# The opening of a two-layer diffusion backbone step: order of the first loads, and three table operations put behind the last modulated x

## Chip, cores and metric

The kernel runs on one core of one Trainium2 chip. The metric is device time in microseconds (us) of one execution; lower is better. A run's time is the span of the profiled work plus what lies around it.

## The reference, cut to what matters

Each layer first makes a modulation out of a condition vector, six vectors of 1024 (shift, scale, gate, twice), and applies shift and scale to its input:

```python
def modulation(cond, w, b):
    return jnp.split((jax.nn.silu(cond) @ w + b)[:, None, :], 6, axis=-1)

mp = modulation(c_ctx[None, :], w_ada[l], b_ada[l])   # 128 prompt tokens
ms = modulation(c, w_ada[l], b_ada[l])                # 256 latent tokens
hp = xp * (1 + mp[1]) + mp[0]
hs = xs * (1 + ms[1]) + ms[0]
# layer 0: windowed attention and a bidirectional recurrence behind one projection of h
... = jnp.split(h @ w_in, EVEN_SPLIT, axis=-1)
```

In layer 0 queries and keys of the latent tokens are rotated with a table of cosines and sines (`rope`); in layer 1 the same rotation follows an RMS norm with the gains `d_q_norm` and `d_k_norm`. Everything is float32; d_model is 1024, there are 384 tokens, and `w_ada` is 1024 x 6144 a layer.

## The kernel before, in words

h is kept with the features on the partitions, in eight blocks of 128 features, each as a high part `hH` and a low part `hL` (float32r), and each weight tile is split in the same way (`wload`, lines 113 to 124: ACT writes `wh` on line 122, DVE writes `wl` on line 123). A product is then three matmuls.

**The opening (function `mixer_ab`, lines 979 to 1070).** Before anything can be projected, shift and scale of layer 0 must exist. That is done in four steps u = 0..3, each for 256 of the 1024 features:

- `ada_first(u)` (lines 293 to 317) is a generator. Up to its first `yield` it issues eight loads of 256 KB of `w_ada` (line 299), into four tiles of a ring of five (`raws`). Then TensorE makes 64 small products with the transposed condition `cT` (line 307), in portions of 32, 16 and 16; DVE adds the bias (`ada_row`, line 311); TensorE transposes the row (`ada_t`, line 314); DVE writes shift and scale into `modT` (lines 316, 317).
- `x_load(hf)` (line 990) loads a half of x (512 features of 3 x 128 tokens) in three transfers; `x_turn(k0, k1)` (line 996) transposes a block of 128 features with three transposes on TensorE (line 1000) and copies the result out, even blocks on ACT (line 1004), odd ones on DVE (line 1002).
- `h_part(u)` (line 1009) writes `hH` (ACT, line 1015), the unrounded h (DVE, line 1016) and `hL` (DVE, line 1018) of two blocks.
- `proj_load(u)` and `proj_part(u, i, js)` (lines 1022, 1027) load three tiles of `w_in_ab` and add to six accumulators; six matmuls a call (lines 1036 to 1038).

In the loop over u the parts of the projection of step u stand alternately with the portions of `ada_first(u + 1)`: the first part, 32 products, the second, 16, the third, 16 and the row, the fourth, then the transposed row; the last two parts behind it. In the kernel before, the second half of x is loaded and transposed in step u = 0.

**What sets the order.** Inside `tc.manual_schedule(engines={ET.SP, ET.PE})` the instructions of SP's queue and of TensorE stay in the order of the program. ACT, DVE and POOL are ordered by a planner that simulates a timeline when the kernel is built; `ahead(part)` gives it a priority offset (`"rope": 1000`). On the chip each engine works off its queue in order, and an instruction that waits holds up all behind it. Every load is issued by SP.

**The tables.** Behind the loop, `load_consts` (line 138) loads the sink logits, norm gains and the rotation tables, and makes `nsink` (DVE, line 144); `load_masks` (line 149) loads the band mask and rounds it into `bmaskR` (ACT, line 155) and casts `lmask` (POOL). `fold_rope` (line 1209) multiplies the rotation table with a gain for layer 1 (DVE, lines 1214 and 1216: `tb`, with `gdk`); it is called at line 1469 with the priority of `"rope"`, and its first result is read in layer 1.

**The start.** Lines 82 to 95 load the identity and both condition vectors, take the SiLU on ACT (line 87), transpose on TensorE and copy to `cT` on DVE (line 91). ACT loads a function table ahead of the rounding of `ident` (line 151) and another one ahead of the SiLU.

Of the kernel before, what the change touches and what calls it, by code (L numbers as in the profile page):

```python
# [9 lines left out]
F32 = mybir.dt.float32  # L10
F32R = mybir.dt.float32r
U8 = mybir.dt.uint8
AF = mybir.ActivationFunctionType
ALU = mybir.AluOpType
# [6 lines left out]
P = 128  # L21
D = 1024
# [19 lines left out]
def tile_backbone_step(ctx, tc, I, O):  # L42
    nc = tc.nc
# [30 lines left out]
    dma = nc.sync.dma_start  # L74

    @contextmanager
    def ahead(part, more=0):
        with tc.high_priority(offset=AHEAD[part] + more):
            yield


    ident = const.tile([P, P], F32, name="ident")
    dma(out=ident, in_=I["k_ident"])
    cond = adas.tile([P, 256], F32, tag="row", name="cond")[0:16, 0:P]
    dma(out=cond[0:8, :], in_=I["c_ctx"].rearrange("(k p) -> k p", p=P))
    dma(out=cond[8:16, :], in_=I["c"].rearrange("a (k p) -> (a k) p", p=P))
    nc.scalar.activation(cond, cond, AF.Silu)
    p0 = psa.tile([P, 512], F32, tag="psa", name="p_cond")
    nc.tensor.transpose(p0[:, 0:16], cond, ident[0:16, 0:16])
# [2 lines left out]
        out=cT, in_=p0[:, 0:16].rearrange("p (c k) -> p k c", c=2).unsqueeze(2).to_broadcast([P, KD, 16, 2]))  # L92
# [8 lines left out]
    hH = const.tile([P, KD, NTOK], F32R, name="hH")  # L101
    hL = const.tile([P, KD, NTOK], F32R, name="hL")
# [33 lines left out]
    C = {}  # L136

    def load_consts():
        for name, ap, n in (("sink", I["a_sink"], 8), ("gnorm", I["b_gnorm"], P), ("gckv", I["c_kv_norm"], 256),
                            ("gdq", I["d_q_norm"], 64), ("gdk", I["d_k_norm"], 64)):  # L140
            C[name] = const.tile([P, n], F32, name=name)
            dma(out=C[name], in_=ap.to_broadcast([P, n]))
        C["nsink"] = const.tile([P, 8], F32, name="nsink")
        nc.vector.tensor_scalar(out=C["nsink"], in0=C["sink"], scalar1=-1.0, scalar2=None, op0=ALU.mult)
        for name, sh in (("rope", [P, 2, 2, 64]), ("ropec", [P, 2, 2, 32])):
            C[name] = const.tile(sh, F32, name=name)
            dma(out=C[name], in_=I["k_" + name])

    def load_masks(stg, pool):
        C["identR"] = pool.tile([P, P], F32R, name="identR")  # L150
        nc.scalar.activation(C["identR"], ident, AF.Copy)
        C["bmask"] = pool.tile([P, 2, P], F32R, name="bmaskR")
        bmask = stg([P, 2, P], F32, "bmask")
        dma(out=bmask, in_=I["k_band"])
        nc.scalar.activation(C["bmask"], bmask, AF.Copy)
        C["lmask"] = pool.tile([P, 7, P], U8, name="lmask")
        for a, b in ((0, 4), (4, 7)):
            lm32 = stg([P, b - a, P], F32, "lm32")
            dma(out=lm32, in_=I["k_lmask"][:, a:b, :])
            nc.gpsimd.tensor_copy(out=C["lmask"][:, a:b, :], in_=lm32)  # L160
# [655 lines left out]
    def mixer_ab():  # L816
# [4 lines left out]
        M = Slots(es, {"one": (1, 0), "pr": (4, 768), "pt": (6, 512), "qS": (2, 1536), "qf": (3, 768),  # L821
                       "X": (8, 768), "at": (2, 768), "vB": (2, 768), "kq": (3, 768), "t2": (5, 512),
                       "gB": (1, 1536)})
# [162 lines left out]
        xh = {}  # L986
        xq = [M.tile("qS", F32).rearrange("p (u j n) -> p u j n", u=2, j=2) for _ in range(2)]
        xT = [xq[u // 2][:, u % 2] for u in range(4)]

        def x_load(hf):  # L990
            for t in range(3):
                xh[t, hf] = M.tile("pt", F32)
                src = I["x_prompt"][0] if t == 0 else I["x_sample"][0, (t - 1) * P:t * P]
                dma(out=xh[t, hf], in_=src[:, hf * 512:(hf + 1) * 512])

        def x_turn(k0, k1):
            for k in range(k0, k1):
                tp = pst("xtp")
                for t in range(3):
                    nc.tensor.transpose(tp[:, t * P:(t + 1) * P], xh[t, k // 4][:, (k % 4) * P:(k % 4 + 1) * P], ident)  # L1000
                if k % 2:
                    nc.vector.tensor_copy(out=xT[k // 2][:, k % 2, :], in_=tp[:, :NTOK])
                else:
                    nc.scalar.activation(xT[k // 2][:, k % 2, :], tp[:, :NTOK], AF.Copy)
# [4 lines left out]
        def h_part(u):  # L1009
            for j in range(2):  # L1010
                k = 2 * u + j
                h32 = M.sm.tile([P, NTOK], F32, tag="sg", name="h32")
                for cnd, sl in ((0, slice(0, P)), (1, slice(P, NTOK))):
                    sc, sh = modT[0][:, 1, u, j, cnd:cnd + 1], modT[0][:, 0, u, j, cnd:cnd + 1]
                    nc.scalar.activation(hH[:, k, sl], xT[u][:, j, sl], AF.Identity, bias=sh, scale=sc)
                    nc.vector.tensor_scalar(out=h32[:, sl], in0=xT[u][:, j, sl], scalar1=sc, scalar2=sh,
                                            op0=ALU.mult, op1=ALU.add)
                nc.vector.tensor_tensor(out=hL[:, k, :], in0=h32, in1=hH[:, k, :].bitcast(F32), op=ALU.subtract)

        w0 = {}  # L1020

# [15 lines left out]
                    nc.tensor.matmul(a, wl, hH[:, kk, :], start=False, stop=False)  # L1037
                    nc.tensor.matmul(a, wh, hL[:, kk, :], start=False, stop=(kk == KD - 1))

        bias = M.tile("pr", F32)[:, 0:512].rearrange("p (u n) -> p u n", u=4)  # L1040
        with tc.manual_schedule(engines={ET.SP, ET.PE}):
            x_load(0)
            ada = ada_first(0, raws, bias)
            next(ada)
            for g in range(4):
                src = I["b_ada"][0:1, (g // 2) * D:(g // 2 + 1) * D].rearrange("a (u j n) -> a u j n", u=4, j=2)
                dma(out=bias[32 * g:32 * g + 32], in_=src[:, :, g % 2, :].to_broadcast([32, 4, P]))
            x_turn(0, 4)
            for _ in ada:
                pass  # L1050
            for u in range(4):
                proj_load(u)
                if u == 0:
                    x_load(1)
                ada = ada_first(u + 1, raws, bias) if u < 3 else iter(())
                next(ada, None)
                h_part(u)
                for i, j in ((0, 0), (0, 1), (1, 0), (1, 1), (2, 0)):
                    proj_part(u, i, (j,))
                    if u == 0 and i < 2:  # L1060
                        x_turn(4 + 2 * i + j, 5 + 2 * i + j)
                    if i < 2:
                        next(ada, None)
                if u == 3:
                    load_vecs()
                next(ada, None)
                proj_part(u, 2, (1,))
            load_consts()
            stg = lambda sh, dt, n: M.tile("t2", dt)[:, 0:sh[1] * sh[2]].rearrange("p (a b) -> p a b", a=sh[1])
            load_masks(stg, M.one)  # L1070
# [379 lines left out]
    for l in range(2):  # L1450
        if l == 0:
            ps, first = mixer_ab()
        else:
            keep = ctx.enter_context(tc.tile_pool(name="keep", bufs=4))
            ps, first = mixer_cd(ps, acc)
        ms = mod_scalars(l, 1)
        with tc.tile_pool(name="bnd", bufs=1) as b1:
            x_t = [b1.tile([P, D], F32, name=f"x{t}") for t in range(3)]
            acc, *part = ffn_parts(l)
            boundary(b1, x_t, l, 0, lambda k: hH[:, k, :], lambda k: hL[:, k, :], ORDER[l], I["w_out"][l], lambda: ms,  # L1460
                     x_in if l == 0 else x_mid, False, first, lvt if l == 0 else None, part)
            with tc.tile_pool(name="part", bufs=1) as pp, tc.tile_pool(name="ffn", bufs=1) as fp:
                kept = [keep.tile([P, 2, 512], F32R, tag="k4", name="k4") for _ in range(4)] if keep else []
                n = 22 - len(kept)
                aH, aL = [[fp.tile([P, NTOK], F32R, name=f"{a}{i}") for i in range(n - 1, -1, -1)][::-1] +
                          [x[:, i, 0:NTOK] for x in kept] for i, a in enumerate(("aH", "aL"))]
                if l == 0:
                    with ahead("rope"):
                        tbk, tbq = fold_rope("gdk", True), fold_rope("gdq", False)
                ada_todo.extend(ada_steps(*a, pp, l) for a in ADA[l][1])  # L1470
                ps = ffn(l, acc, ps)
                ms2 = mod_scalars(1, 0) if l == 0 else None
                acc, *part = cd_parts() if l == 0 else (None, None)
                boundary(b1, x_t, l, 1, lambda k: aH[k], lambda k: aL[k], list(range(22)), I["w_ffn_down"][l],
                         lambda: ms2, None, l == 1, nxt_part=part)
# [49 lines left out]
```

## Time and profile before

| | us |
|---|---|
| median of 3 runs (1102.97 to 1103.16) | 1103.03 |
| the profiled execution's own time | 1102.89 |
| its span | 1100.9 |

| engine | busy us | share of the span | instructions |
|---|---|---|---|
| PE (matmul) | 1038.8 | 94% | 6105 |
| PEld (weight load) | 874.3 | 79% | 6105 |
| DVE | 661.4 | 60% | 1140 |
| ACT | 443.4 | 40% | 805 |
| POOL | 119.2 | 11% | 166 |

A busy time is the sum over the engine's instructions; PE and PEld overlap. The 94% is a mean over the whole span, and the stages differ: the opening is the first 66 us. A wait is named by what ended last before the waiting instruction began.

### The profile page before, as it was taken

How to read it: one execution, taken by the hardware profiler on the slowest of the kernel's cores; microseconds unless marked ns; L12 is line 12 of the kernel's file. 1: busy time of each engine (PE TensorE's matmuls, PEld its weight loads, DVE VectorE, ACT ScalarE, POOL GpSimd, SP SyncE). 2: the span in 40 equal slices, each digit the busy share in tenths (PEclk: the TensorE clock that was granted, in tenths of full speed). 3: DMA queues.
4: the chain of work that ended last, by engine and by line, in shares of the span. 5: the costliest groups of instructions: out<-in, count | busy, mean ns of one | idle time of the engine just before them, and what ended most of it. 6: DMA issues, size and time to landing. Idle time of an engine off the chain costs nothing. (4 is left out here: it accounts for less than half of the span.)

```text
span 1100.9 us, 15874 instructions
## 1 busy us (share of the span) xinstructions
PE 1038.8 (94%) x6105; PEld 874.3 (79%) x6105; DVE 661.4 (60%) x1140; ACT 443.4 (40%) x805; POOL 119.2 (11%) x166
## 2 busy tenths in 40 slices
PE   5899999996999999999999998979899999999996
PEld 4688867565789989898778786666589999998885
DVE  2476754677498548458326975765489464343237
ACT  2364744464153333332222546646354333333231
POOL 0021200200110000000000343212130000000004
PEclk8999999998899999999999999999999999999998
DMA  9865244475137776766655432144126455543331
GB/s 284 257 197 154 71 147 125 136 251 176 50 115 227 222 250 210 240 205 212 239 196 160 138 112 66 35 139 163 48 86 180 148 175 151 171 123 126 134 115 58
DMA packets 113553, 173.12 MB, mean 157 GB/s; under 512 B 9387, under 2 KB 80582, under 8 KB 113478
## 3 DMA queue, kind: packets, MB, share of 16 engines
q1 hardware_dynamic: 113478, 172.11, 49.7%
q8 instruction: 48, 0.79, 0.3%
q14 instruction: 27, 0.22, 0.1%
HBM read 167.84 MB, written 4.24 MB: 156 GB/s over the span
## 5 line engine op out<-in xcount | busy, mean ns | idle before, releaser
L123 DVE TENSOR_TENSOR wl<-wr,wh 128x1024 fp32r<-128x1024 f32 (+4 forms) x200 | 235.8, 1182 | 227.6 <-ACT wh L122 224.9
L122 ACT ACTIVATE wh<-wr 128x1024 fp32r<-128x1024 f32 (+4 forms) x200 | 202.5, 1015 | 344.4 <-PE pf L128 119.9
L127 PE MATMUL pf<-hH,wh 128*128 128x384 f32 x688 | 232.7, 338 | 0.0
L129 PE MATMUL pf<-hH,wl 128*128 128x384 f32 x688 | 232.7, 338 | 0.0
L128 PE MATMUL pf<-hL,wh 128*128 128x384 f32 x688 | 232.6, 338 | 0.0
L129 PEld LDWEIGHTS pf<-hH,wl 128*128 128x128 f32 x688 | 129.4, 188 | 3.1 <-issue 3.1
L128 PEld LDWEIGHTS pf<-hL,wh 128*128 128x128 f32 x688 | 129.4, 188 | 2.7 <-issue 2.6
L127 PEld LDWEIGHTS pf<-hH,wh 128*128 128x128 f32 x688 | 129.4, 188 | 2.3 <-issue 2.2
L127 PE MATMUL o<-wh,aH 128*128 128x512 f32 (+1 forms) x280 | 101.3, 362 | 0.4 <-DVE a L1171 0.4
L128 PE MATMUL o<-wl,aH 128*128 128x512 f32 (+1 forms) x280 | 101.2, 361 | 0.1
L129 PE MATMUL o<-wh,aL 128*128 128x512 f32 (+1 forms) x280 | 101.0, 361 | 0.0
L129 PE MATMUL pj<-wh,hL 128*128 128x512 f32 (+3 forms) x240 | 89.1, 372 | 1.7 <-POOL hL L342 1.5
L127 PE MATMUL pj<-wh,hH 128*128 128x512 f32 (+3 forms) x240 | 89.2, 377 | 0.0
L128 PE MATMUL pj<-wl,hH 128*128 128x512 f32 (+3 forms) x240 | 89.1, 372 | 0.0
L259 DVE SCALAR_TENSOR_TENSOR part<-ar,cT,part 128x512 f32<-128x512 f32 x112 | 80.3, 746 | 14.3 <-DMA ar<-in_w_ada 14.2
L110 POOL TENSOR_TENSOR ve<-ve,nhalf 128x1 f32<-128x1 f32 x12 | 7.0, 583 | 618.4 <-DVE ve L528 356.8
L127 PEld LDWEIGHTS o<-wh,aH 128*128 128x128 f32 x280 | 52.9, 189 | 10.1 <-issue 1.4
L129 PEld LDWEIGHTS o<-wh,aL 128*128 128x128 f32 x280 | 52.8, 188 | 9.1 <-issue 1.2
L128 PEld LDWEIGHTS o<-wl,aH 128*128 128x128 f32 x280 | 52.9, 189 | 8.5 <-DVE wl L123 0.4
L129 PEld LDWEIGHTS pj<-wh,hL 128*128 128x128 f32 x240 | 45.1, 188 | 11.9 <-POOL hL L342 2.4
L127 PEld LDWEIGHTS pj<-wh,hH 128*128 128x128 f32 x240 | 44.8, 188 | 9.8 <-issue 2.3
L128 PEld LDWEIGHTS pj<-wl,hH 128*128 128x128 f32 x240 | 45.2, 188 | 8.5 <-issue 1.8
(319 smaller groups left out, 1550.2 us busy)
## 6 DMA issues: line engine op xcount, KB each, us to landing
ar<-in_w_ada SPq DMA_DIRECT2D x80, 512.0 KB
wr<-in_w_ffn_down SPq DMA_DIRECT2D x44, 512.0 KB
wr<-in_w_ffn_gate SPq DMA_DIRECT2D x40, 512.0 KB
wr<-in_w_ffn_up SPq DMA_DIRECT2D x40, 512.0 KB
wr<-in_w_in_ab SPq DMA_DIRECT2D x18, 512.0 KB
ar<-in_w_ada SPq DMA_DIRECT2D x32, 256.0 KB
wr<-in_w_out SPq DMA_DIRECT2D x16, 512.0 KB
wr<-in_w_in_ab SPq DMA_DIRECT2D x16, 256.0 KB
```

Of the source, the lines that this page charges most:

```text
L110: nc.gpsimd.tensor_tensor(out=out, in0=v, in1=nhalf[:, :n], op=ALU.pow)
L122: nc.scalar.activation(hi, raw, AF.Copy)
L123: nc.vector.tensor_tensor(out=lo, in0=raw, in1=hi.bitcast(F32), op=ALU.subtract)
L127: nc.tensor.matmul(out, lh, rh, start=start, stop=False)
L128: nc.tensor.matmul(out, lh, rl, start=False, stop=False)
L129: nc.tensor.matmul(out, ll, rh, start=False, stop=stop)
L259: nc.vector.scalar_tensor_tensor(out=dst, in0=raw[:, j], scalar=sc, in1=dst, op0=ALU.mult, op1=ALU.add)
```

## The change

- `ident` and the two condition vectors are loaded by instructions of ACT's queue (`nc.scalar.dma_start`) instead of SP's; so are the four pieces of the bias, which now stand ahead of the section whose order is fixed.
- SP's first loads are those of `ada_first(0)`; x follows.
- x comes in quarters of 256 features, two transfers each (prompt; both latent tiles together), into tiles of tag `pr`; the bias takes a tile of tag `pt`. Quarter u + 1 is loaded in step u, behind `proj_load(u)`, and transposed in step u at the third and fourth part of the projection (two blocks a step, for u = 0, 1, 2). The first quarter's two blocks are transposed behind the products of `ada_first(0)` and ahead of its `ada_t`.
- `nsink` and `fold_rope` on DVE may stand in the queue only behind the last `hL`, `bmaskR` on ACT only behind the last `hH` (`tc.issue_after`, an order of the queue on one engine, with no semaphore).

```diff
     ident = const.tile([P, P], F32, name="ident")
-    dma(out=ident, in_=I["k_ident"])
+    nc.scalar.dma_start(out=ident, in_=I["k_ident"])
     cond = adas.tile([P, 256], F32, tag="row", name="cond")[0:16, 0:P]
-    dma(out=cond[0:8, :], in_=I["c_ctx"].rearrange("(k p) -> k p", p=P))
-    dma(out=cond[8:16, :], in_=I["c"].rearrange("a (k p) -> (a k) p", p=P))
+    nc.scalar.dma_start(out=cond[0:8, :], in_=I["c_ctx"].rearrange("(k p) -> k p", p=P))
+    nc.scalar.dma_start(out=cond[8:16, :], in_=I["c"].rearrange("a (k p) -> (a k) p", p=P))
...
-        nc.vector.tensor_scalar(out=C["nsink"], in0=C["sink"], scalar1=-1.0, scalar2=None, op0=ALU.mult)
+        with tc.issue_after(C["h0"].ins):
+            nc.vector.tensor_scalar(out=C["nsink"], in0=C["sink"], scalar1=-1.0, scalar2=None, op0=ALU.mult)
...
-        nc.scalar.activation(C["bmask"], bmask, AF.Copy)
+        with tc.issue_after(C["h1"].ins):
+            nc.scalar.activation(C["bmask"], bmask, AF.Copy)
...
-        def x_load(hf):
-            for t in range(3):
-                xh[t, hf] = M.tile("pt", F32)
-                src = I["x_prompt"][0] if t == 0 else I["x_sample"][0, (t - 1) * P:t * P]
-                dma(out=xh[t, hf], in_=src[:, hf * 512:(hf + 1) * 512])
+        def x_load(u):
+            xh[u] = M.tile("pr", F32).rearrange("p (t n) -> p t n", t=3)
+            sl = slice(u * 256, (u + 1) * 256)
+            dma(out=xh[u][:, 0, :], in_=I["x_prompt"][0][:, sl])
+            dma(out=xh[u][:, 1:3, :], in_=I["x_sample"][0].rearrange("(t p) n -> p t n", p=P)[:, :, sl])
...
-                    nc.scalar.activation(hH[:, k, sl], xT[u][:, j, sl], AF.Identity, bias=sh, scale=sc)
+                    C["h1"] = nc.scalar.activation(hH[:, k, sl], xT[u][:, j, sl], AF.Identity, bias=sh, scale=sc)
...
-                nc.vector.tensor_tensor(out=hL[:, k, :], in0=h32, in1=hH[:, k, :].bitcast(F32), op=ALU.subtract)
+                C["h0"] = nc.vector.tensor_tensor(out=hL[:, k, :], in0=h32, in1=hH[:, k, :].bitcast(F32), op=ALU.subtract)
...
-        bias = M.tile("pr", F32)[:, 0:512].rearrange("p (u n) -> p u n", u=4)
+        bias = M.tile("pt", F32).rearrange("p (u n) -> p u n", u=4)
+        for g in range(4):
+            src = I["b_ada"][0:1, (g // 2) * D:(g // 2 + 1) * D].rearrange("a (u j n) -> a u j n", u=4, j=2)
+            nc.scalar.dma_start(out=bias[32 * g:32 * g + 32], in_=src[:, :, g % 2, :].to_broadcast([32, 4, P]))
         with tc.manual_schedule(engines={ET.SP, ET.PE}):
-            x_load(0)
             ada = ada_first(0, raws, bias)
             next(ada)
-            for g in range(4):
-                src = I["b_ada"][0:1, (g // 2) * D:(g // 2 + 1) * D].rearrange("a (u j n) -> a u j n", u=4, j=2)
-                dma(out=bias[32 * g:32 * g + 32], in_=src[:, :, g % 2, :].to_broadcast([32, 4, P]))
-            x_turn(0, 4)
+            x_load(0)
+            for _ in range(3):
+                next(ada)
+            x_turn(0, 2)
             for _ in ada:
                 pass
             for u in range(4):
                 proj_load(u)
-                if u == 0:
-                    x_load(1)
+                if u < 3:
+                    x_load(u + 1)
...
                 for i, j in ((0, 0), (0, 1), (1, 0), (1, 1), (2, 0)):
                     proj_part(u, i, (j,))
-                    if u == 0 and i < 2:
-                        x_turn(4 + 2 * i + j, 5 + 2 * i + j)
+                    if u < 3 and i == 1:
+                        x_turn(2 * u + 2 + j, 2 * u + 3 + j)
...
-                    with ahead("rope"):
+                    with ahead("rope"), tc.issue_after(C["h0"].ins):
                         tbk, tbq = fold_rope("gdk", True), fold_rope("gdq", False)
```

## Rows read from the trace of the kernel before

**Rows 1.** Busy time by stage; start:end, length, engines, clock, DMA share, GB/s.

```profile
51.00:57.00 6.00, 0.62 (x3) 0.62 (x4) 1.17 (x8) 0.42 (x1) 0.72 (x2) 0.64 0.84 240
60.00:330.00 270.00, 256.50 (x1482) 196.75 (x1481) 182.81 (x375) 135.79 (x282) 38.81 (x49) 0.96 0.45 139
```

**Rows 2.** Waits, first 70 us: who, for whom: us, times, longest.

```profile
PEld ada_t L314 <- DVE ada_row L311: 7.5, 2, 5.9
PE ada_t L314 <- DVE ada_row L311: 6.9, 2, 5.6
...
PEld a L1038 <- DVE hL L1018: 1.1, 4, 0.4
```

**Rows 3.** DVE's timeline, 48 to 57 us: start, duration, instruction, idle time before.

```profile
48.94 0.17 DVE L144 TENSOR_SCALAR nsink<-sink 128x8 f32<-128x8 f32 x1 [1.94 <-DMA sink<-in_a_sink]
49.15 1.22 DVE L123 TENSOR_TENSOR wl<-wr,wh 128x1024 fp32r<-128x1024 f32 x1
55.05 0.23 DVE L1214 TENSOR_TENSOR tb<-rope,gdk 128x64 f32<-128x64 f32 x1 [4.67 <-DMA rope<-in_k_rope]
...
56.04 0.28 DVE L311 TENSOR_TENSOR ada_row<-ada,pr 128x128 f32<-128x128 f32 x1
```

**Rows 4.** TensorE's timeline around the gap and to the next projection.

```profile
48.93 0.65 PE L307 MATMUL ada<-ar,cT 128*32 128x128 f32 x16
...
50.49 0.34 PE L1038 MATMUL a<-hL,wh 128*128 128x384 f32 x1
56.38 0.47 PE L314 MATMUL ada_t<-ident,ada_row 128*128 128x128 f32 x1 [5.55 <-DVE ada_row L311]
56.51 0.67 PE L1036 MATMUL a<-hH,wh 128*128 128x384 f32 x1
...
59.52 0.34 PE L1036 MATMUL a<-hH,wh 128*128 128x384 f32 x1
...
66.40 0.28 PE L127 MATMUL pj<-wh,hH 128*128 128x256 f32 x1
```

**Rows 5.** ACT's timeline around the same gap.

```profile
55.56 0.42 ACT L155 ACTIVATE bmaskR<-t 128x256 fp32r<-128x256 f32 x1 [6.44 <-DMA t<-in_k_band]
...
60.29 0.63 ACT L122 ACTIVATE wh<-wr 128x512 fp32r<-128x512 f32 x1 [0.99 <-ACT hH L1015]
```

**Rows 6.** Timeline of the first 20 us, all engines: the first modulation.

```profile
14.63 0.63 PE L307 MATMUL ada<-ar,cT 128*32 128x128 f32 x12 [0.74 <-DMA ar<-in_w_ada]
...
16.30 0.29 DVE L311 TENSOR_TENSOR ada_row<-ada,pr 128x128 f32<-128x128 f32 x1 [5.59 <-DMA wr<-in_w_in_ab]
...
16.65 0.33 PE L314 MATMUL ada_t<-ident,ada_row 128*128 128x128 f32 x1 [1.39 <-DVE ada_row L311]
...
17.48 1.86 ACT L1015 ACTIVATE hH<-qS,modT 128x128 fp32r<-128x128 f32 x4 [0.20 <-DVE modT L317]
...
18.52 0.69 PE L1036 MATMUL a<-hH,wh 128*128 128x384 f32 x1 [1.54 <-ACT hH L1015]
```

**Rows 7.** SP's timeline: issues of loads.

```profile
0.72 0.39 SPq L83 DMA_DIRECT2D ident<-in_k_ident  x1
...
1.89 0.36 SPq L994 DMA_DIRECT2D pt<-in_x_prompt  x1
...
3.24 4.82 SPq L299 DMA_DIRECT2D ar<-in_w_ada  x8
8.42 2.53 SPq L1047 DMA_DIRECT2D pr<-in_b_ada  x4
```

**Rows 8.** Busy time by stage, in the columns of rows 1.

```profile
0.00:9.00 9.00, 2.44 (x9) 1.83 (x10) 0.55 (x2) 3.67 (x5) 0.54 (x8) 1.00 0.65 198
9.00:11.00 2.00, 2.00 (x26) 1.61 (x28) 0.99 (x2) 0.49 (x1) 0.00 (x0) 1.00 1.10 372
21.00:25.00 4.00, 4.00 (x39) 2.98 (x39) 0.55 (x1) 0.49 (x1) 0.00 (x0) 0.50 1.10 348
```

**Rows 9.** ACT's first instructions.

```profile
0.72 1.28 ACT L151 ACT_TABLE_LOAD   x1 [0.72 <-PEq L1514]
...
4.28 0.31 ACT L87 ACTIVATE cond<-cond 16x128 f32<-16x128 f32 x1
```

**Rows 10.** A block of x on TensorE, and a copy of one on DVE.

```profile
25.89 0.49 PE L1000 MATMUL xtp<-ident,pt 128*128 128x128 f32 x3
...
31.68 0.55 DVE L1002 COPY qS<-xtp 128x384 f32<-128x384 f32 x1
```

More of the change, by code (lines that the diff above doesn't have):

```diff
@@ L999, in x_turn @@
                 for t in range(3):
-                    nc.tensor.transpose(tp[:, t * P:(t + 1) * P], xh[t, k // 4][:, (k % 4) * P:(k % 4 + 1) * P], ident)
+                    nc.tensor.transpose(tp[:, t * P:(t + 1) * P], xh[k // 2][:, t, (k % 2) * P:(k % 2 + 1) * P], ident)
                 if k % 2:
```

## The prediction

> **What bounds the kernel now.** I first looked at how busy TensorE is stage by stage. From 60 us on it is the bound: 256.5 us busy out of 270 in the next stage, with the DMA engines at 0.45 [rows 1]. So time saved in the opening shifts everything behind it forward, unless a load comes late there. The stretch from 51 to 57 us is different: TensorE works 0.62 us out of 6. The list of waits names the cause: `ada_t` waited for `ada_row`, 6.9 us in two waits, the longer one 5.6 [rows 2].
>
> DVE's timeline shows why the row is late. Its products are done by 49.6 (48.93 + 0.65) [rows 4], but DVE, free at 50.37, has a table product ahead of the row in its queue: `tb` waits 4.67 us for the rotation table, begins at 55.05, and the row follows at 56.04 [rows 3]. The table is read in layer 1 only. TensorE, done with the fourth part of the projection at 50.83, stands still until 56.38 [rows 4]. ACT stood in a wait of its own for the band mask until 55.56 [rows 5], hidden behind the other one: without the row there was no shift or scale for it.
>
> The stall costs a second time. The granted clock averaged 0.64 in that stretch [rows 1], half speed at the end. The matmuls from 56.51 to 59.52 are nine intervals of 0.334 us (1.2 GHz); from 59.52 to 66.40 there are 39 matmuls of step 2 and 3 and one small transpose, 0.176 us each (2.4 GHz) [rows 4].
>
> The other loss is the start. The first `hH` begins at 17.48, the first matmul of the projection at 18.52 [rows 6]. Ahead of it TensorE waits for the last tile of `w_ada` (14.63), and `ada_row`, whose products end at 15.26, starts at 16.30, released by a load; the only load it reads itself is the bias, issued behind all of `w_ada` [rows 6, 7].
>
> **The change part by part**, in us of the profiled execution (1102.89, span 1100.9; the median is 0.14 higher).
>
> *1. `tb`, `nsink`, `bmaskR` behind the last modulation.* The row's products end at 49.6, DVE finishes the `wl` at 50.37, and the row takes 0.28; it is done at 50.7, before TensorE wants it at 50.83. So the wait of 5.55 goes. With it go the nine slow intervals: 9 x (0.334 - 0.176) = 1.4. What is late next: the last h follows `ada_t` with 0.83 + 1.04 us to its first matmul (16.65, 17.48, 18.52) [rows 6], while the twelve matmuls left in step 2 take 12 x 0.176 = 2.1, so the high part is in time, and the low part costs up to the 0.4 that it cost at an earlier step [rows 2]. I charge 0.4. Sum: 5.55 + 1.4 - 0.4 = 6.55.
>
> Behind the waits that are moved stand, on ACT and DVE, the splits of the weights of the next projection. ACT's first is at 60.29 [rows 5], for a projection at 66.40 [rows 4]: six us of cover. The table loads stand on SP's queue behind loads that wait for TensorE to free tiles, so they come earlier with it, though not all of the way. I cost this at nothing; a rival prices its loss.
>
> *2. `w_ada` first, small loads on ACT's queue.* SP's first large issue was x at 1.89, `w_ada` followed at 3.24 [rows 7]; now `w_ada` is issued at 0.72. How soon do its 2.1 MB land? With the bias (0.26) and the identity it is 2.43 MB. By the rates of before, 9 us x 198 GB/s = 1.78 MB, and the rest at 372 GB/s, that amount had landed at 10.8 [rows 8]; with large issues 1.2 us earlier it is 9.6. Up to 1.5 us is to be added if the bias, whose pieces are short runs of 512 bytes, takes turns with `w_ada`; between 9.6 and 11.1 I take 10.5, nearer the late end, since all four pieces can now be issued at once.
>
> The Trainium skill (DMA: Bandwidth & Descriptors, section Queues, rings and completion order) says that each DMA engine goes round between the queues that have work, a packet at a time. By that rule the bias comes in amid `w_ada`, the late end holds, and the start gains 0.6 less. No row here can show it, since SP issues all loads. The same page (section Issuing engines are not separate DMA queues) says that a second issuing engine saves only the time of issuing.
>
> Then: the last 16 products (0.63) to 11.1; x's first quarter, 0.39 MB behind `w_ada`, lands at 11.6; two blocks of 0.5 [rows 10] to 12.6; `hH` 0.83 later [rows 6], 13.4 against 17.48: a gain of 4.0. On ACT's side: three issues ahead of the table load in 1.17 (0.72 to 1.89), and up to four more in 2.53 [rows 7], then two table loads of 1.28 each and a rounding of 0.3, so the SiLU goes from 4.28 [rows 9] to between 4.8 and 7.3, and the first products, a transpose and a copy later, to 8.5 at worst. All but 16 of the 64 are then done before the last tile lands, so it costs nothing. If the bias still came late by 1.0 and `w_ada` at 11.1, the gain would be 2.4; with 9.6 it is 4.9.
>
> *3. x in quarters.* Before, four blocks were transposed while TensorE waited anyway and four within the loop; now two and six. Two more blocks of 0.49 [rows 10] on a busy TensorE: -1.0. In steps 1 and 2 a copy of 0.55 on DVE [rows 10] now stands beside `ada_t`, ahead of `modT`: 0 to 0.55 each; I take 0.4, as nothing covers it: -0.8.
>
> *4. The clock in step 0.* From 21 to 25 us TensorE was busy throughout at a granted 0.50 [rows 8]; before the clock fell, it had stood nearly still from 15.26 to 18.52 [rows 6]. In the change, x's blocks and `ada_t` fill 11.6 to 12.9, the projection starts at 14.5, so the idle stretch is half as long, and I take it that the clock stays up: 4.0 us of work shrinks to 2.0. Part of this is lost at once: the first two tiles of the second `w_ada` group lie 2.62 MB behind the first group (x 0.39, weights 0.79, x 0.39, tiles 1.05), 7.5 us at 348 GB/s [rows 8], thus 18.0, while the first part of the projection ends near 16.9. That leaves 2.0 - 1.1 = 0.9 (bounds 0 and 2.0).
>
> Sum: 6.55 + 4.0 - 1.0 - 0.8 + 0.9 = 9.65. 1102.89 - 9.65 = 1093.2; to the median add 0.14: **1093.4 us**.
>
> **The rivals.**
>
> - *The clock falls as before.* The gaps are sparse until the first low parts are ready, and I can't tell how near the fall is. Then 4 gives nothing: 1094.3. Chance 0.24.
> - *The tables now hold the next projection.* Place: ACT behind the last `hH`, DVE behind the last `hL`. If the table loads land no sooner than before (55.0 to 55.6 [rows 3, 5]), since their own many short pieces set their pace, then band mask, split of the weights on ACT and DVE follow (0.42, 0.63, 0.69) and the projection can start at 57.7 and goes on haltingly, where the forecast has 66.4 - 9.65 = 56.7: a loss of 1 to 3, 1096. Chance 0.12. **Slower than before** by the same mechanism: each us that the tables land later costs one; the gain is gone when they land past 64, and the kernel is over 0.2% slower from 66 on, say 1106. For it: all their issues were strung out behind slow small loads. Against it: SP issues them earlier. Chance 0.05.
> - *Part of the gain is given back.* The planner orders ACT, DVE and POOL anew from other start times; the 13.5 us that TensorE idles between 60 and 330 [rows 1] could grow. Half of the gain gone is 1098.2; chance 0.10. Nearly all gone, within 0.2%: 0.04.
> - *The order does not bite*, because another waiting instruction takes `tb`'s place ahead of the row. Then only 2 to 4 count, 3.1 us: 1099.9. Chance 0.05.
>
> **How the numbers follow.** The forecast has the rest, 0.40. The bounds of the unknown costs: at best 6.95 + 4.9 - 1.0 + 2.0 = 12.85, that is 1090.2; at worst 6.55 + 2.4 - 1.0 - 1.1 = 6.85, that is 1096.2. With the table rival (3 off) and part of the give-back the range reaches 1099; below, 1090. About 2 in 10 lie outside. Faster by over 0.2% (2.2 us, about what a measurement of this kernel can tell from no change): 0.91; within it 0.04; slower 0.05.
>
> **What would show it.** Right: `tb`, `nsink` and `bmaskR` stand behind the last h in their queues; no wait of `ada_t` over 1.5 us; granted clock near 1.00 at the last step; first `hH` near 13.4, the next projection (line 127) near 56.7. Wrong: a first `hH` after 15.5, so that ACT's issues or the bias decide; a wait of line 127's matmuls for `wl` or `wh`; a granted 0.50 in step 0; or TensorE idling longer behind 60 us than in the kernel before.

## The result, and the profile after

| | before | changed |
|---|---|---|
| median of 11 runs each, us | 1104.63 (1102.83 to 1108.02) | 1097.79 (1091.89 to 1102.80) |
| ratio, 95% interval | | 0.9934 [0.9912, 0.9955] |
| profiled execution, us | 1102.89 | 1095.94 |
| its span, us | 1100.9 | 1094.1 |

The change is faster by 0.66%, 7.3 us on the 1103.03 shown (5.0 to 9.7 by the interval); the forecast was 9.65. TensorE's work is the same and its share of the span rises to 95% (the page's first part, after):

```profile
PE 1036.0 (95%) x6105; PEld 870.7 (80%) x6105; DVE 660.6 (60%) x1140; ACT 440.8 (40%) x804; POOL 120.0 (11%) x166
```

Stages of the changed kernel, in the columns of [rows 1] and [rows 8]:

```profile
51.00:57.00 6.00, 5.88 (x33) 5.17 (x32) 3.41 (x14) 4.02 (x8) 1.52 (x2) 1.00 0.95 292
60.00:330.00 270.00, 256.93 (x1475) 196.48 (x1474) 186.53 (x381) 132.50 (x280) 39.31 (x49) 0.96 0.46 141
15.00:21.00 6.00, 3.79 (x30) 2.77 (x34) 3.49 (x9) 2.81 (x5) 0.00 (x0) 0.50 1.10 349
...
0.00:9.00 9.00, 1.58 (x27) 1.38 (x31) 0.42 (x1) 1.79 (x3) 0.54 (x8) 1.00 0.78 224
```

The stretch from 51 to 57 us, in which TensorE had worked 0.62 us, is now full (5.88, at a granted 1.00). From 15 to 21 us the granted clock is 0.50 all the same. The 270 us behind 60 us show the same load as before (256.93 us busy against 256.50). TensorE's timeline, to be held against [rows 4] and [rows 6]:

```profile
17.02 0.69 PE L1038 MATMUL a<-hH,wh 128*128 128x384 f32 x1 [3.78 <-ACT hH L1017]
...
30.80 0.34 PE L1038 MATMUL a<-hH,wh 128*128 128x384 f32 x1
...
40.94 0.41 PE L1038 MATMUL a<-hH,wh 128*128 128x384 f32 x1
...
51.41 0.41 PE L1038 MATMUL a<-hH,wh 128*128 128x384 f32 x1
...
58.76 0.36 PE L127 MATMUL pj<-wh,hH 128*128 128x256 f32 x1
```

The first matmuls of the four steps and of the next projection start at 17.02, 30.80, 40.94, 51.41 and 58.76; in the kernel before they started at 18.52, 33.58, 43.44, 60.04 and 66.40. So the gain can be taken apart by stretch, and the forecast's terms too (its x blocks: two fewer in step 0, two more in each of steps 1 and 2):

| stretch | before | after | gain forecast | gain measured |
|---|---|---|---|---|
| start to step 0 | 18.52 | 17.02 | 4.0 | 1.5 |
| step 0 | 15.06 | 13.78 | 1.0 + 0.9 = 1.9 | 1.3 |
| step 1 | 9.86 | 10.14 | -1.0 - 0.4 = -1.4 | -0.3 |
| step 2 | 16.60 | 10.47 | 6.95 - 1.4 = 5.55 | 6.1 |
| step 3 to the next projection | 6.36 | 7.35 | -0.4 | -1.0 |
| sum | 66.40 | 58.76 | 9.65 | 7.6 |

The largest loss against the forecast, 2.5, lies in the first row; the rows of steps 1 and 2 won back 1.7 of it. What stands between `ada_t` and the first `hH` there (all engines, 11.5 to 17.1 us):

```profile
12.97 0.27 PE L316 MATMUL ada_t<-ident,ada_row 128*128 128x128 f32 x1
13.11 0.63 ACT L122 ACTIVATE wh<-wr 128x512 fp32r<-128x512 f32 x1 [6.05 <-DMA wr<-in_w_in_ab]
...
13.77 0.69 DVE L123 TENSOR_TENSOR wl<-wr,wh 128x512 fp32r<-128x512 f32 x1 [1.34 <-ACT wh L122]
14.38 0.55 DVE L1004 COPY qS<-xtp 128x384 f32<-128x384 f32 x1
14.85 0.15 DVE L318 COPY modT<-ada_t 128x8 f32<-128x8 f32 x1
...
15.04 1.06 ACT L122 ACTIVATE wh<-wr 128x1024 fp32r<-128x1024 f32 x1 [0.92 <-DMA wr<-in_w_in_ab]
...
16.00 1.35 ACT L1017 ACTIVATE hH<-qS,modT 128x128 fp32r<-128x128 f32 x3
```

`modT` could be written at 13.2, when `ada_t` is there, but starts at 14.85. On DVE a weight split (13.77) and a copy of x (14.38) stand ahead of it, and that split waits for ACT's, which waited 6.05 us for its load. On ACT the large split (15.04), which waited for a load as well, stands ahead of `hH`. From `ada_t` to `hH` it is 3.03 us where [rows 6] had 0.83. In the kernel before, the small split on DVE and the large one on ACT stood behind `hH` (17.48), and the planner has changed their order:

```profile
18.66 0.69 DVE L123 TENSOR_TENSOR wl<-wr,wh 128x512 fp32r<-128x512 f32 x1
19.25 1.04 ACT L122 ACTIVATE wh<-wr 128x1024 fp32r<-128x1024 f32 x1
```

### The profile page after: what moved, and what is told of

Read it like the earlier page. It is cut to its first block, busy times and chain, and to the rows that moved or that the text cites. A ratio compares the mean times of both kernels' runs of the same rounds, so it can differ in the third digit from the quotient of the medians.

```text
span 1094.1 us, 15881 instructions
## 1 busy us (share of the span) xinstructions
PE 1036.0 (95%) x6105; PEld 870.7 (80%) x6105; DVE 660.6 (60%) x1140; ACT 440.8 (40%) x804; POOL 120.0 (11%) x166
```

## The experiments

Times are medians; ratios are to runs of the kernel before on the same chip. The start of the next projection (line 127) in the profiled run is given as "pj". No kernel here leaves work out; two add transposes that nobody reads.

**1. The edges alone.** The kernel before with the three `issue_after` lines, no other part of the change.

```diff
+        with tc.issue_after(C["h0"].ins):   (nsink; fold_rope likewise)
+        with tc.issue_after(C["h1"].ins):   (bmaskR)
```

> The kernel before with nothing but the three order edges (nsink and the rotation-table products behind the last hL, bmaskR behind the last hH); loads as before. Theory A, the edges carry the bulk: the 5.55 us gap before ada_t of the last step goes and with it the slow clock behind it; the projection of line 127 starts near 60 (before 66.4, after 58.8) and the time falls by 5.5 to 7 us. Theory B, the earlier loads carry half or more: the time falls by under 4 us.

```profile
60.02 0.36 PE L127 MATMUL pj<-wh,hH 128*128 128x256 f32 x1 [0.47 <-DVE vT L174]
```

Measured: 1098.10, ratio 0.9931 [0.9907, 0.9955]; pj 60.02 (-6.4), first `hH` 17.1, only one wait of `ada_t` left, 1.2 at the start. The edges carry 6.4 of the 7.6 us at pj, about the size of the forecast's first step (6.55), and in time as much as the whole change (0.9934), as far as the intervals tell the two apart.

**2. The loads alone.** The changed kernel without the edges.

```diff
-        with tc.issue_after(...):           (nsink, bmaskR, fold_rope: back as before)
```

> The changed kernel without the three order edges: loads, quarters and ACT's issues alone. Theory A: DVE again has nsink and the table products ahead of the last row, so TensorE stands from about 49.2 until the rotation table has landed (near 53.5) and the row follows, over 4.5 us, with the clock at half behind it; the gain at the line-127 projection is 1 to 3 us and so is the gain in time. Theory B: the gap is at most 1 us because the table loads land earlier too, and the gain is 5 us or more.

Measured: 1102.65, ratio 0.9984 [0.9970, 0.9998]; pj 66.43, where the kernel before has 66.40. TensorE, ACT and DVE around the stall:

```profile
54.34 0.90 PE L1000 MATMUL xtp<-ident,pr 128*128 128x128 f32 x3 [5.56 <-ACT qS L1004]
...
55.44 0.48 PE L314 MATMUL ada_t<-ident,ada_row 128*128 128x128 f32 x1 [0.20 <-DVE ada_row L311]
...
60.52 0.41 PE L1036 MATMUL a<-hH,wh 128*128 128x384 f32 x1
...
66.43 0.28 PE L127 MATMUL pj<-wh,hH 128*128 128x256 f32 x1
...
53.49 0.42 ACT L155 ACTIVATE bmaskR<-t 128x256 fp32r<-128x256 f32 x1 [6.97 <-DMA t<-in_k_band]
53.82 0.47 ACT L1004 ACTIVATE qS<-xtp 128x384 f32<-128x384 f32 x1
...
53.03 0.22 DVE L1216 TENSOR_TENSOR tb<-rope,gdk 128x64 f32<-128x64 f32 x1 [6.32 <-DMA rope<-in_k_rope]
```

TensorE waits 5.56 us again, now for a copy of x: ACT has the band mask ahead of it. The steps ahead were earlier by some 2.5 us, and all of it is lost, in three parts. The tables land 2.0 us sooner (`tb` 53.03 against 55.05, `bmaskR` 53.49 against 55.56 [rows 3, 5]), not 2.5. Behind the landing the copy of x, a weight split and the last block of x come ahead of `ada_t`, which starts 0.9 sooner than before (55.44 against 56.38). And the low pace then lasts for fifteen intervals (55.57 to 60.52, 0.33 us each) where the kernel before had nine, which costs the last 0.9. So theory A is right about the stall, but not about its engine (it named DVE alone) nor about the 1 to 3 us that were to be left at pj.

**3. Only the band mask free again.** The changed kernel without the edge of `bmaskR`.

```diff
-        with tc.issue_after(C["h1"].ins):
-            nc.scalar.activation(C["bmask"], bmask, AF.Copy)
+        nc.scalar.activation(C["bmask"], bmask, AF.Copy)
```

> The changed kernel with bmaskR's order edge alone taken out; DVE's two stay. Theory A, a second stall is hidden behind the first: ACT waits for the band mask (lands near 54) ahead of the last copy of x and the last hH, so TensorE stops near 51 until about 55.5, the projection of line 127 starts 4 us or more later than in the changed kernel, and 4 to 6 us of the gain are lost. Theory B, the mask is off the path: same time as the changed kernel within 1 us.

```profile
54.77 0.90 PE L1001 MATMUL xtp<-ident,pr 128*128 128x128 f32 x3 [5.63 <-ACT qS L1005]
...
47.96 0.29 DVE L312 TENSOR_TENSOR ada_row<-ada,pt 128x128 f32<-128x128 f32 x1
...
53.92 0.42 ACT L156 ACTIVATE bmaskR<-t 128x256 fp32r<-128x256 f32 x1 [7.17 <-DMA t<-in_k_band]
```

Measured: 1104.24, ratio 1.0006 [0.9984, 1.0028]; pj 66.44. The row is there at 47.96, early, and the whole gain is gone: ACT's wait alone holds TensorE for 5.63 us.

**4. Only DVE's edges off.** The counterpart: `bmaskR` stays behind the last `hH`, `nsink` and `fold_rope` are free.

```diff
-        with tc.issue_after(C["h0"].ins):   (nsink)
-                    with ahead("rope"), tc.issue_after(C["h0"].ins):
+                    with ahead("rope"):
```

> The changed kernel without the two edges on DVE (nsink, fold_rope), with the one on ACT (bmaskR): the counterpart of the run that freed the mask alone. Theory (two stalls stand side by side, one on ACT and one on DVE, and either is enough): ada_t waits 5 or more for ada_row at about 54, the next projection at 65.5 to 66.5, time 1102 to 1104. Rival (only ACT's wait counts in the changed kernel, because row and tables now meet in another order on DVE): no wait of ada_t over 1.5, projection at 58 to 60, time 1097 to 1099.

```profile
55.55 0.47 PE L315 MATMUL ada_t<-ident,ada_row 128*128 128x128 f32 x1 [6.31 <-DVE ada_row L312]
...
53.13 0.23 DVE L1217 TENSOR_TENSOR tb<-rope,gdk 128x64 f32<-128x64 f32 x1 [6.27 <-DMA rope<-in_k_rope]
```

Measured: 1105.30, ratio 1.0025 [1.0005, 1.0046]; pj 65.80. In the changed kernel two stalls stand side by side, one on each engine, of 5.63 and 6.31 us, and each is enough by itself. Neither ACT's edge nor DVE's two gained anything measurable without the other.

**5. The first weights behind the modulation.** In step 0 the small split on DVE is put behind `modT`, the large one on ACT behind `hH`; ACT's small one (14.45) stays ahead.

```diff
+            with tc.issue_after(C["m"].ins):          # C["m"]: the last write of modT
+                a = wload(w[ks, 768:1024], 2, 256, part="w0")
+                with tc.issue_after(C["h1"].ins):
+                    w0[u] = (a, wload((w[ks, 1792:2048], w[ks, 2304:2560]), 2, 512, part="w0"))
```

> The changed kernel with the weight split of step 0 put behind the first modulation: on DVE both wl behind modT, on ACT the large wh behind the first hH. Theory A, the queue order on DVE and ACT holds the first h: hH starts near 14.1 instead of 16.0, the first matmul of the projection near 15.2 instead of 17.0, and if the clock then stays up, 1 to 3 us off the changed kernel's time. Theory C, the loads set the pace: the first h comes earlier but TensorE waits the same time later for w_ada of step 1 or its weights, and the line-127 projection starts within 0.5 us of the changed kernel's.

```profile
14.59 0.42 PE L316 MATMUL ada_t<-ident,ada_row 128*128 128x128 f32 x1
...
15.31 0.15 DVE L318 COPY modT<-ada_t 128x8 f32<-128x8 f32 x1
...
15.76 1.86 ACT L1017 ACTIVATE hH<-qS,modT 128x128 fp32r<-128x128 f32 x4 [0.30 <-DVE modT L319]
```

Measured: 1097.05, ratio 0.9924 [0.9902, 0.9945]; pj 58.0. The distance from `ada_t` to `hH` is 1.17 instead of 3.03, so the two splits were the reason for the distance. But here the second part of x landed for 13.46 where the changed kernel had it for 12.37, `ada_t` is 1.6 later, and `hH` comes only 0.24 sooner. With the splits out of the way, the loads bound the start. Neither expectation came whole: `hH` near 14.1 was not reached, and pj is 0.8 ahead of the changed kernel (0.3 ahead of run 6).

**6. The changed kernel once more**, on another chip, beside the next three kernels.

> The changed kernel itself, as the yardstick of the three beside it on the same chip: 5 to 9 us faster than before; ada_t to the first hH about 3.0 us, matmuls of step 0 at 0.32 us each (1.2 GHz) until some 22 us.

Measured: 1098.09, ratio 0.9940 [0.9919, 0.9962]; pj 58.3, first `hH` 16.2: the opening repeats within 0.5 us.

**7. The splits out of the way in all steps.** As 5; in steps 1 to 3 the large `wl` goes behind `modT`, and all copies of x go to ACT.

```diff
-                if k % 2:
-                    nc.vector.tensor_copy(out=xT[k // 2][:, k % 2, :], in_=tp[:, :NTOK])
-                else:
-                    nc.scalar.activation(xT[k // 2][:, k % 2, :], tp[:, :NTOK], AF.Copy)
+                nc.scalar.activation(xT[k // 2][:, k % 2, :], tp[:, :NTOK], AF.Copy)
```

> The split of the weights behind the first modulation in step 0, the large wl behind modT in the later steps too, and all copies of x on ACT, so that DVE has nothing but the row and modT in the chain. Theory A, the queue order on DVE holds each step: ada_t to hH falls from about 3.0 to 1.2 us in step 0 and the wait of ada_t at the end of step 0 (1.2 us) goes; the line-127 projection starts 1 to 2.5 us earlier than in the changed kernel and the time falls by as much. Theory C, loads set the pace: under 0.7 us.

Measured: 1095.50, ratio 0.9916 [0.9900, 0.9933]; first `hH` 14.9, pj 58.1. Of a start that is 1.1 earlier only 0.7 is left at pj (against run 6, on the same chip, 0.2 of 1.3), less than the 1 us or more of theory A; TensorE's waits up to 60 us name the reason:

```profile
PE a L1044 <- DVE hL L1017: 2.5, 3, 0.8
PE a L1042 <- ACT hH L1014: 2.1, 1, 2.1
```

In the later steps the large `wl` now stands between `modT` and h on DVE, and the low parts are late by 0.82 three times. The same kernel again, beside number 10:

> e6 once more, on the chip of e9, to compare the two. If e6's lead over the changed kernel is real (2.3 us in the fast runs so far), this run gives 1094.5 to 1097 and an interval that ends below 0.995; if it was scatter, 1097 to 1099.

Measured: 1097.98, ratio 0.9951 [0.9930, 0.9971]; first `hH` 14.6, pj 57.2. The lead over the changed kernel in time is within the scatter.

**8 and 9. TensorE kept busy ahead of the products.** 16 transposes of the identity in front of the condition's, once in kernel 7 and once in the changed kernel.

```diff
+    for _ in range(16):
+        nc.tensor.transpose(p0[:, P:2 * P], ident, ident)
```

> As the previous one, with 16 transposes of the identity into an unused part of a PSUM tile ahead of the transpose of the condition, so that TensorE is busy from about 3 to 7 us. Theory D, the first products and step 0 run at 1.2 GHz because TensorE did nothing ahead of them: the 64 products then take 0.034 us each as far as their tiles have landed, step 0's matmuls are 0.17 us apart from the start, and the line-127 projection starts a further 1.5 to 3 us earlier. Theory C: the products wait for w_ada and step 0 for the next tiles, and under 0.7 us comes of it.

> The changed kernel with the 16 transposes alone. Theory D: step 0 at 0.17 us a matmul, but the first hH still held by the weight split ahead of modT (about 3 us from ada_t to hH), in which time the clock may fall again: 0 to 2.5 us faster than the changed kernel. Theory C: no difference.

Measured: 1099.31, ratio 0.9957 [0.9938, 0.9977], pj 57.6; and 1098.00, ratio 0.9936 [0.9912, 0.9961], pj 58.8. The second one's products:

```profile
7.67 1.08 PE L311 MATMUL ada<-ar,cT 128*32 128x128 f32 x32 [0.52 <-DVE cT L93]
9.47 0.41 PE L311 MATMUL ada<-ar,cT 128*32 128x128 f32 x4 [0.72 <-DMA ar<-in_w_ada]
10.67 2.49 PE L311 MATMUL ada<-ar,cT 128*32 128x128 f32 x28 [0.79 <-DMA ar<-in_w_ada]
```

The first 32 take 1.08, full pace, and then wait for tiles; the end, at 13.1, is no earlier than without the transposes (12.0), since the last tile is used from 12.09 (11.24 without). The loads set it. In run 9 the granted clock is 0.50 from 11 to 23 us, and in run 8 from 17 to 19, where the matmuls stand 0.32 apart. So neither run had step 0 at 0.17 from the start, as theory D wanted; run 8's pj is 0.5 ahead of run 7's, not 1.5 to 3, and run 9's is where the changed kernel has it.

**10. The large split last.** As 7, but the large `wl` goes behind the last `hL` in every step.

```diff
-                with tc.issue_after(C["m"].ins):
+                with tc.issue_after(C["h0"].ins):
                     w0[u] = (a, wload(big, 2, 512, part="w0"))
+                C["h0"] = C["wl"]
```

> e6 with one more shift: in every step the large wl stands behind the last hL on DVE instead of ahead of h (step 0: the large wh behind the last hH on ACT, as before). Theory E (what is left in the opening is order on DVE alone): the three waits of TensorE for hL of 0.82 in e6 fall to 0.45 or less, no wait for wl takes their place above 0.3, the next projection starts near 57.0 (e6 58.1), and the time is 1094.5. Rival F (a wait for the large wl takes their place: it is needed twelve matmuls, 2.1 us, behind the first one): a wait of 0.5 to 1.2 per step for wl at the third part of the projection, the projection at 58 to 59, time 1095.5 to 1096.5.

Measured: 1096.33, ratio 0.9939 [0.9915, 0.9962], profiled run 1093.39; first matmul 16.06, pj 56.2, 1.0 ahead of kernel 7 on the same chip. The waits for `hL` are gone from TensorE's list up to 60 us, which has one line left behind 15 us:

```profile
PE a L1044 <- ACT hH L1014: 1.5, 1, 1.5
```

This is the earliest pj of all, earlier than theory E had it (57.0), but its time of 1094.5 did not come. Yet of 2.6 us ahead of the changed kernel 1.1 remain at the first output projection (187.2 against 188.3, below), and the interval does not separate the two times. What is late instead, TensorE behind 60 us:

```profile
64.66 0.44 PE L794 MATMUL tk<-ident,t 128*128 128x128 f32 x2 [1.34 <-ACT sg L845]
```

The timeline leads from there back to a load: the function table for this `sg` waits for `X` on DVE (61.89), in whose queue a weight split (60.43) stands ahead, and that waited for ACT's `wh` (59.76), which waited 1.92 us for its weights. In the changed kernel the wait for `sg` is 0.68, in run 6 it is 0.23. No run here moves that load.

**11. The bias on SP's queue again**, behind the first quarter of x.

```diff
-            nc.scalar.dma_start(out=bias[32 * g:32 * g + 32], ...)   (ahead of the ordered section)
+                dma(out=bias[32 * g:32 * g + 32], ...)               (behind x_load(0))
```

> The changed kernel, with the four loads of the bias issued by SP again, behind the first quarter of x. Theory (the bias, issued by ACT, takes turns with the first weights of the modulation and holds SiLU up): SiLU starts at 4.3 to 4.8 instead of 6.55, the last tile of w_ada is there 0.4 to 0.7 sooner (products behind the last wait at 10.5 to 10.8 instead of 11.24), x in proportion; but the row then waits for the bias (behind x and ahead of the weights of the projection, about 1 us), so that ada_t stays at 12.5 to 13.5, and the first hH at 15 to 16.5, since the large weight still stands ahead of it. Time 1097 to 1099, next projection within 0.5 of 58.8. Rival (the bias costs nothing beside the weights): the last tile comes at 11.1 to 11.4 as before, the row later by what the bias takes on SP's queue, first hH 16.5 to 17.5.

Measured: 1097.49, ratio 0.9942 [0.9921, 0.9962]; pj 60.0, outside the 58.3 to 59.3 that was expected. The weight loads of the products, here and in the changed kernel, show the last wait for `w_ada`:

```profile
60.01 0.36 PE L127 MATMUL pj<-wh,hH 128*128 128x256 f32 x1 [1.62 <-DVE vT L174]
...
10.25 0.61 PEld L309 LDWEIGHTS ada<-ar,cT 128*32 128x32 f32 x12 [0.20 <-DMA ar<-in_w_ada]
```

```profile
11.24 0.52 PEld L309 LDWEIGHTS ada<-ar,cT 128*32 128x32 f32 x12 [0.52 <-DMA ar<-in_w_ada]
```

The last tile comes 1.0 us sooner when the bias is not beside it; in the eleven profiled runs with the bias on ACT's queue it is used from 11.24 to 12.09. But the row then waits for the bias to 13.56, `hH` starts at 16.38 instead of 16.00, and the start wins nothing. The late pj is another matter: it waits 1.62 for `vT`, a copy behind other work in DVE's queue. SiLU moved only from 6.55 to 6.14, so the expected 4.3 to 4.8 was wrong: its function table's load waited for the condition vectors to 4.85 in this order as well.

## Why the prediction was right, and where it was off

The forecast, 1093.4 and faster, held in direction, and the median lies inside the range; the gain was 7.3 instead of 9.65. The first step is shown by runs 1 to 4. The others were never run apart; what they are worth is read from the table by stretch. That the sum came within 2.4 us is in part luck: x, charged too dear, covers two thirds of what the start lost. Two of the forecast's own signs of being wrong came, a first `hH` after 15.5 (16.00, by the weight splits and not by ACT's issues or the bias) and a granted 0.50 in step 0. By its steps:

1. **`tb`, `nsink`, `bmaskR` behind the last modulation** (6.55): right in mechanism and size. The edges alone gave 6.4 at pj, and step 2 gained 6.1 net of its two blocks of x. The late low part was charged with 0.4 and cost 0.7 (step 3's first eight matmuls take 1.91 us from start to start, 51.41 to 53.32, where 0.173 each would make 1.2). ACT's wait, "hidden behind the other one", has a price of its own where DVE's part alone is moved: run 3 shows it, 5.63, in the changed kernel, where a copy of x stands behind the mask; in the kernel before `hH` does, and no run has its price there. That the change moved it too is what made the sum come out.
2. **`w_ada` first** (4.0): the term that was mis-sized; it measured 1.5. At 224 GB/s 2.0 MB had landed by 9 us, and the last tile was used from 11.24 (taken: landed at 10.5, bounds 9.6 to 11.1); `ada_t` started at 12.97 (12.6). So 0.4 went there, and 2.2 in "`hH` 0.83 later": that distance was copied from [rows 6], where DVE's split and ACT's large one stood behind `hH` (18.66, 19.25). The planner, from its own start times, put them ahead, where they wait for their loads. That the planner orders anew was a rival for the time behind 60 us; it happened here, at 13 us. Run 5 brings the distance back to 1.17. The bounds (2.4 to 4.9) did not hold this case, because they priced loads alone and not the order of the two queues. By the rule that the forecast took from the Trainium skill (DMA: Bandwidth & Descriptors, section Queues, rings and completion order), the engines going round between the queues, the bias would come in amid `w_ada` and make the last tile late. Run 11 agrees: 11.24 with the bias beside it, 10.25 without; from 6 to 10 us the engines are as busy in both (shares 1.01 to 1.12), but move 258 to 305 GB/s with it and 338 to 370 without. SP's eight issues also took 6.50 us with it and 4.09 without, so the trace does not tell late issues from shared engines. No row gave the 1.5 us that the late bound allowed for this; the runs put it at 1.0 to 1.8.
3. **x in quarters** (-1.8): too dear. Steps 1 and 2 were charged with 2.8 for two blocks and a copy each; step 1 grew by 0.3, and step 2, 16.60 less the 6.95 of the stall, from 9.65 to 10.47, by 0.8. The two blocks took 0.74 and 0.75 of TensorE's time instead of 1.0. The copy, charged with 0.4 a step, holds `modT` up by just that (`modT` at 39.42 and 49.89, `ada_t` done at 39.01 and 49.49). But its price falls due as late low parts at the start of the step behind, steps 2 and 3. At the start of step 1 the kernel before paid it as well: DVE's copy at 31.68 stands ahead of `modT` (32.15) there, and TensorE waits 0.71 at 33.58. The changed kernel has no such wait at 30.80: its copy at 28.41 runs while the row is transposed (28.55). The forecast left that out.
4. **The clock stays up in step 0** (0.9): wrong. The granted clock is 0.50 from 15 to 21 us, as in the first rival; the matmuls stood 0.32 apart until some 21.8 us. TensorE had waited 3.78 us ahead of 17.02, where the forecast had it idle for 1.6 (12.9 to 14.5). But the splits are not the whole of it. With them out of the way TensorE waits 1.79, 2.13 and 1.54 us there (runs 5, 7, 10), and part of step 0 still runs at half pace: at 0.32 us a matmul until 23.2 us in run 5 and until 22.1 in run 10, at a granted 0.50 from 18 to 21 in run 7. So the step that failed is "half as long, and I take it that the clock stays up"; what would keep it up stays open. Step 0 still gained 1.3: it has two blocks of x less, the low pace ended sooner (at 21 to 25 us the kernel before was at 0.50 [rows 8]), and a wait of 0.7 for `hH` at its end is gone, while one of 1.2 for `ada_row` has come.

Of the rivals, the one by which **the tables hold the next projection** did not come about. Behind the last h, TensorE wants nothing at once that waits for the tables:

```profile
52.24 0.56 DVE L1020 TENSOR_TENSOR hL<-h,hH 128x384 fp32r<-128x384 f32 x1 [0.17 <-ACT hH L1017]
53.68 0.23 DVE L1218 TENSOR_TENSOR tb<-rope,gdk 128x64 f32<-128x64 f32 x1 [0.88 <-DMA rope<-in_k_rope]
...
54.16 0.42 ACT L157 ACTIVATE bmaskR<-t 128x256 fp32r<-128x256 f32 x1 [1.95 <-DMA t<-in_k_band]
```

They land 1.4 us sooner than before (53.68 and 54.16 against 55.05 and 55.56 [rows 3, 5]); DVE waits 0.88 for them, ACT 1.95, and the projection behind starts some 0.3 late, which the 7.6 at pj contains. Of the rival by which **part of the gain is given back** 1.0 came about: 7.6 at pj, 6.6 at the first output projection. TensorE waits 0.68 for `tk` and 0.18 behind it there, and in the kernel before it had no such wait. Whether ACT's 1.95 for the mask come out again in the 0.68 is not shown; in run 10 ACT waited 0.60 for the mask, and `tk` waited 1.34. **The order does not bite** fell with run 1.

Behind that the runs scatter. The first `o` of layer 0, before and after (columns: durations, first and last start):

```profile
L127 PE MATMUL o<-wh,hH x112: 281/394/776, 194.9 to 810.2; 128*128 128x512 f32 x80, 128*128 128x256 f32 x32
```

```profile
L127 PE MATMUL o<-wh,hH x112: 281/393/793, 188.3 to 803.0; 128*128 128x512 f32 x80, 128*128 128x256 f32 x32
```

It starts at 194.9 in the profiled runs of the kernel before and of runs 2 and 3, at 194.1 in run 4, and at 187.0 to 189.9 where both stalls are gone. From there to the end of the span the 14 profiled runs took 903.8 to 910.6 us, with no clear order by kernel, so a single pair of runs does not tell a difference of some us. The start of `o` does: in the changed kernel and its repeat, run 6, it is 188.3 and 187.6.

## What to carry to other kernels

A stall that ends with a landing keeps of a gain ahead of it no more than the landing itself moves, and what stands behind it in the queues and a low clock after it can take that too (run 2). Two such stalls on different engines hide one another: move every waiting instruction of that kind, and test each alone and all together. When the order of loads changes, list anew, for each in-order queue on the path, what stands between the producer and its consumer and which load that waits for: a planner may have changed that too, and a distance copied from the old trace holds only for the old order. Where times scatter by some us, compare the start of an operation behind the change.

## What the runs showed of the hardware that was not expected

- The granted-clock column can say 1.00 where the matmuls run at half pace: in run 10 it reads 1.00 from 18 to 21 us (in runs 2, 3 and 5 from 17 to 20), and the matmuls of 384 columns stand 0.32 us apart, as they do in the changed kernel under a granted 0.50. At the start, the spacing of the matmuls is to be read beside it.

```profile
18.00:21.00 3.00, 3.00 (x35) 1.90 (x34) 1.09 (x1) 0.00 (x0) 0.00 (x0) 1.00 1.10 349
```

```profile
17.69 0.52 PE L1044 MATMUL a<-hH,wh 128*128 128x384 f32 x1
18.01 0.52 PE L1045 MATMUL a<-hH,wl 128*128 128x384 f32 x1
18.33 0.52 PE L1046 MATMUL a<-hL,wh 128*128 128x384 f32 x1
```

- Loads issued by ACT take time of its queue, 0.30 to 0.89 us each (the two of the bias at 2.13 together 1.78). The SiLU moved from 4.28 [rows 9] to 6.55, but not by the time of those issues: its function table's load waits to 5.25 for the condition vectors, which were issued by 2.10. In the kernel before, where they were issued ahead of the large loads, that load began at 2.99 without a wait. The products had slack for it here.

```profile
0.72 0.43 ACTq L83 DMA_DIRECT2D ident<-in_k_ident  x1
...
1.80 0.30 ACTq L86 DMA_DIRECT2D cond<-in_c  x1
2.13 1.78 ACTq L1045 DMA_DIRECT2D pt<-in_b_ada  x2
5.25 1.28 ACT L87 ACT_TABLE_LOAD   x1 [5.25 <-DMA cond<-in_c]
...
6.55 0.31 ACT L87 ACTIVATE cond<-cond 16x128 f32<-16x128 f32 x1
```
